# Factors prepared one ring entry at a time, and last sums that go on from copies in their banks

## The chip, the cores and the metric

The kernel runs on one core of one Trainium2 chip. The metric is the time of one execution on the device in microseconds (us). TensorE (PE in the profile, PEld its weight loads) multiplies matrices into PSUM, which has eight banks of 128 partitions by 512 float32; VectorE (DVE) and ScalarE (ACT) do elementwise work; SyncE (SP) issues the loads from HBM into SBUF.

## The reference

A decoder trunk of two layers over 256 positions, width 2048, all in float32: layer 0 mixes with a gated short convolution, layer 1 with latent attention of 16 heads. Behind each mixer stands an MLP with a squared ReLU, and every sub-layer is followed by a layer norm of the scaled input plus its result. What matters here are the two MLPs and the last norm:

```python
def sq_relu_mlp(x, w1, w2):
    return jnp.square(jax.nn.relu(x @ w1)) @ w2
...
    h = layer_norm(ALPHA * h + mix, ln_g[layer, 0], ln_b[layer, 0])
    h = layer_norm(ALPHA * h + sq_relu_mlp(h, mlp_w1[layer], mlp_w2[layer]), ln_g[layer, 1], ln_b[layer, 1])
```

w1 is 2048 x 8192 and w2 is 8192 x 2048 in each layer.

## The kernel before

**Factors and their ring.** A weight is used as two parts, hi and lo: ScalarE rounds the float32 value to float32r (hi), VectorE subtracts (lo = value - hi), and TensorE multiplies with both. split (L127, L128) does this for one *unit* of 128 x 1024 values. Units live in a ring of eight (the pool whl, tags hi and lo, WA = 8); the raw values are loaded into a ring of five (raws, RAW = 5; each load is issued at L138 on SP's queue). A unit of either ring can be filled again when its last reader has finished.

**The stream.** All weights stand in one list, stream, in the order of use. A *plain* entry is one unit: one load, one hi, one lo. A *paired* entry serves seven products that stand for eight (a Strassen scheme on two by two blocks) and is three units, prepared by prepare(i) in this order: unit 1 from the first load; unit t from differences of the two loads (raw_t, L160; its parts are hi_t and lo_t); unit 2 from the second load after L163 has put a difference into half of it; and then a half unit t4 (L166 and a split into t) in buffers of its own. FACTORS gives the order of the seven products (numbered 3, 1, 5, 7, 2, 6, 4): the first two read unit 1, the next two unit t, the next two unit 2, the last t4. Each is one dot: three matmuls at L290, L292 and L293, of which L292 reads lo.

**How far ahead.** take() hands out the next entries and first prepares those ahead, as long as their units, counted from the entries handed out, come to no more than LOOK = 5 (in one place LOOK + 1). It is called in the order of the program, ahead of the matmuls that use the entry. What is called earlier in the program is ranked higher, but the order of the instructions in each engine's queue is fixed when the kernel is built, by a planner that plays the program through with its own estimates: among the instructions that are ready at its time on an engine it takes the one that stands first in the program. In the queue each engine then keeps that order.

**One MLP.** The 8192 hidden columns are done in eight stages q of eight chunks of 128 (m = 0 to 7). In each, products computes x @ w1 for the chunks (names ps_u, L205 and L209), hidden applies ReLU and square (whole, L348; L704, L705) and splits the result into h; then the stage's part of h @ w2 follows. In q = 0 and q = 7 that is down (ps_d): all plain entries. In q = 1 to 6, the *fast* stages, it is down_pairs: three paired entries s0, s1, s2, then two plain ones p0 and p1 (all of these into ps_r), then four paired entries f0 to f3 (into ps_f). forms holds the sums of h blocks that the paired products need.

**Sums.** The running sums of h @ w2 lie in SBUF (acc, and sums for the four products named in OWN). In a fast stage a sum is copied into its bank by ScalarE (resumed, L605), TensorE accumulates onto it, and ScalarE copies it back (put_back, L609). Around the end of p1 these copies stand in the program so: put_back of the products 1, 5, 7 and 6 and resumed of 3 and 1 before the call of take for p0; resumed of 5 and 7 and put_back of 2 and 4 between that call and the call for p1; put_back of 22 and 3 behind the matmuls of p1. In q = 1 the four products of OWN start anew, so that resumed makes no copy for them. At q = 7 fold adds sums into acc while products runs.

**The end.** In q = 7 of the last MLP, down does the output blocks n = 0 and 1 and down_late the blocks 2 and 3, first for the rows t = 0, then for t = 1. For each (n, t) the bank is added to block(n, t) of acc (put, L592); finished then takes statistics of the row (bn_stats, L1025) and, after the last block, normalises: mean, variance and its root, centred (L1039), scaled (L1042), and for t = 1 three offsets from TensorE (L1053, L1058), whose banks Banks.next() draws from a count modulo eight. store sends the result to HBM.

Of the kernel before, what the change touches and what calls it, by code (L numbers as in the profile page):

```python
# [22 lines left out]
NQ = 8  # L23
# [11 lines left out]
NB = 4  # L35
# [18 lines left out]
def trunk(ctx: ExitStack, tc: tile.TileContext, xT, vecs, lead, w_first, w_in, w_out, w_kv, w_q, w_uk, w_uv,  # L54
# [66 lines left out]

    state = {"split": 0, "next": 0}
    ready = {}
# [17 lines left out]
    def prepare(i):  # L141

        if len(stream[i]) == 1:
            raw = load_raw(i, stream[i][0])
            hi, lo = ready[i] = parts(i)
            split(hi, lo, tiled(raw))
            return
        r1, r2 = (load_raw(f"{i}_{j}", src) for j, src in enumerate(stream[i]))
        out = []

        def finished(r, name):
            hi, lo = parts(name)
            split(hi, lo, tiled(r))
            out.append((hi, lo))

        b22, (b21, b12) = r1[:, BW:], (r2[:, :BW], r2[:, BW:])
        finished(r1, f"{i}_1")
        t = raws.tile([P, 1024], F32, tag="raw", name=f"raw{i}_t")
        two = "p (a c) -> p a c"
        nc.vector.tensor_tensor(t.rearrange(two, a=2), b12.unsqueeze(1).to_broadcast([P, 2, BW]),  # L160
                                r1.rearrange(two, a=2), ALU.subtract)
        finished(t, f"{i}_t")
        nc.vector.tensor_tensor(b12, b22, t[:, :BW], ALU.subtract)  # L163
        finished(r2, f"{i}_2")
        t4 = r1[:, :BW]
        nc.vector.tensor_tensor(t4, b21, b12, ALU.subtract)  # L166
        f = state["fast"].tile([P, 2, BW], F32R, tag="t4", name=f"t4_{i}", bufs=2)
        split(f[:, 0, :], f[:, 1, :], t4)
        b1, t13, b2 = ([[v.rearrange("p b c -> p (b c)")[:, o:o + BW] for v in w] for o in (0, BW)] for w in out)
        ready[i] = {"11": b1[0], "22": b1[1], "21": b2[0], "T2": b2[1], "T1": t13[0], "T3": t13[1],  # L170
                    "T4": [f[:, 0, :], f[:, 1, :]]}

    def size(i):

        return 1 if len(stream[i]) == 1 else 3

    def take(halves=2, look=LOOK):

        i = state["next"]
        state["next"] += halves  # L180
        ahead = -sum(size(j) for j in range(i, i + halves))
        for j in range(i, len(stream)):
            ahead += size(j)
            if ahead > look:
                break
            if j >= state["split"]:
                prepare(j)
                state["split"] = j + 1
        return [ready.pop(i + j) for j in range(halves)]

# [111 lines left out]

    def down(x, put, n, banks=(None, None), amid=None):

        ps = [psum("ps_d", bank) for bank in banks]
        for j in range(len(x) // 2):
            w, = take(1)
            for kk in range(2):
                k = 2 * j + kk
                for t in range(2):  # L310
                    dot(ps[t], wide_rows(w, kk), held(x[k], t), k == 0, k == len(x) - 1)
            if amid and 2 * j + 2 == len(x) // 2:
                amid()
        for t in range(2):
            put(n, t, ps[t])

    def down_late(x, put, blocks):

        ws = {}
        for t in range(2):  # L320
            for n in blocks:
                ps = psum("ps_d")
                for k in range(len(x)):
                    if (n, k // 2) not in ws:
                        ws[n, k // 2], = take(1)
                    dot(ps, wide_rows(ws[n, k // 2], k % 2), held(x[k], t), k == 0, k == len(x) - 1)
                put(n, t, ps)
# [196 lines left out]
    for k0, k1 in pieces:  # L524
# [5 lines left out]
        for u in range(HEAD):  # L530
            hi, lo = ready[2 * u + half]
            split(hi[:, at, :], lo[:, at, :], w[:, :, u, :])
    state["split"] = 2 * HEAD
    nc.sync.dma_start(vec, vecs)
# [32 lines left out]

    def mlp(idx, ln, blocks, fast, begin=None, extra=None):

# [92 lines left out]
        def fold():  # L662
# [3 lines left out]
            for d, a, b in ((c[:, 0, 0], c[:, 0, 0], s1), (s6, s6, s1), (c[:, 0, 1], c[:, 0, 1], s6), (s7, s7, s6),  # L666
# [3 lines left out]
                yield  # L670

        busy, free = (0, 1, 2, 3), (4, 5, 6, 7)
        for q in range(NQ):
# [54 lines left out]
            else:  # L728
                folds = fold()
                begun = {}  # L730
                for m, ps in enumerate(products(QC, xhl, TURNED, busy)):
# [6 lines left out]
                    if q == NQ - 1:  # L738
                        next(folds, None)
                        if begin:  # L740
                            begin(range(max(2 * m, 1), 2 * m + 2))

            if q == NQ - 1:
                blocks(block, put, h)
                return
# [261 lines left out]

    def to_out(block, put, h):
        gbt = act.tile([P, NB, 2 * BW], F32, tag="b", name="gbt")
# [13 lines left out]
        def finished(n, t, ps):  # L1023
            put(n, t, ps)
            nc.vector.bn_stats(out=stats[:, t, n, :], in_=block(n, t))  # L1025
            if n < NB - 1:
                if t == 1:
                    nc.vector.tensor_tensor(block(n, t), block(n, t), gbt[:, n, :BW], ALU.mult)
                return
# [7 lines left out]
            def centred(i):  # L1037
                us[i] = scratch(i)
                nc.vector.scalar_tensor_tensor(us[i], block(i, t), mv[:, 0:1], gbt[:, i, :BW], ALU.subtract, ALU.mult)  # L1039

# [22 lines left out]
        for n in range(2):  # L1063
            down(h, finished, n)
        down_late(h, finished, range(2, NB))

    with tc.tile_pool(name="fast2", bufs=1) as fast:
        mlp(3, after, to_out, fast, extra=turn_residual)
    Banks.close(banks)
# [94 lines left out]
```

## Time and profile before

| | |
|---|---|
| median of 3 runs (lowest to highest) | 2004.91 us (2004.71 to 2005.23) |
| the profiled execution, its own time | 2005.16 us |
| its span, first to last instruction | 2003.4 us |
| mean granted TensorE clock | 0.999 |
| busy share: PE, PEld, DVE, ACT | 100%, 87%, 86%, 67% |
| one fast stage, products of q = 3 to products of q = 4 | 83.65 us (621.65 to 705.30) |
| last matmul into the sums to the end of the span | 11.2 us (from 1992.24) |

A row of a profile view names line, engine, operation and tiles as out<-in; the number behind x is a count, and an arrow in brackets gives the idle time of the engine just before and what ended it. Rows in order of time begin with the start and the duration in us; where several alike follow one another they are merged (x3). Rows of stretches give the bounds, the length, and the busy time of each engine with its number of instructions.

### The profile page before, as it was taken

Reading aid. Unit: us, or ns where it says so; the run is one execution under the profiler, and the core shown is the slowest. Engines: PE = TensorE matmul, PEld = TensorE weight load, DVE = VectorE, ACT = ScalarE, POOL = GpSimd, SP = SyncE. Lnnn points to the kernel's source line nnn. Section 1 sums busy time; section 2 is a strip of 40 time slices with the busy share of each in tenths; the row PEclk is TensorE's granted clock in tenths of the full one; section 3 lists DMA queues with packets and bytes.
Section 4 is the critical chain, followed back from the end, with each engine's and each line's share of the span. In section 5 each row is a group of like instructions: output and inputs, shape, how many; then the busy total and the mean of one; then the engine's idle time right before and its main releaser. Section 6 shows DMA issues by size and latency. Waiting matters only on the chain.

```text
span 2003.4 us, 30132 instructions
## 1 busy us (share of the span) xinstructions
PE 1993.4 (100%) x11114; PEld 1737.5 (87%) x11114; DVE 1715.7 (86%) x2565; ACT 1347.5 (67%) x2142; POOL 2.3 (0%) x21
## 2 busy tenths in 40 slices
PE   9999999999999999999999999999999999999998
PEld 8888888988888888888889998898888888888886
DVE  8667667788999999989978988777899999999986
ACT  6444445586877787877756755558677778887771
POOL 0000000000000000000000000000000000000000
PEclk9999999999999999999999999999999999999999
DMA  8666666564647465574854543656464646656483
GB/s 314 210 189 188 188 190 189 184 193 146 223 164 244 147 231 197 187 247 133 281 173 158 170 140 128 195 183 196 147 233 147 233 159 219 218 181 231 152 276 118
DMA packets 106851, 385.84 MB, mean 193 GB/s; under 512 B 11856, under 2 KB 12624, under 8 KB 106448
## 3 DMA queue, kind: packets, MB, share of 16 engines
q1 hardware_dynamic: 106560, 383.79, 58.8%
q8 instruction: 87, 1.43, 0.3%
q14 instruction: 60, 0.49, 0.1%
q10 hardware_dynamic: 144, 0.13, 0.0%
HBM read 381.78 MB, written 2.10 MB: 192 GB/s over the span
## 4 chain that ended last, share of the span: by engine, by line
PE 90%; DVE 7%; issue 2%; ACT 1%; DMA 0%; DVEq 0%
PE ps_u L205 21%; PE ps_l L205 13%; PE ps_u L209 11%; PE ps_l L209 7%; PE ps_r L292 4%; PE ps_r L290 4%; PE ps_r L293 4%; PE ps_d L292 3%; PE ps_d L290 3%; PE ps_d L293 3%; DVE lo L128 2%; PE ps_w L239 2%; PE ps_w L238 2%; DVE lo_t L128 2%; PE ps_w L237 2%
## 5 line engine op out<-in xcount | busy, mean ns | idle before, releaser
L128 DVE TENSOR_TENSOR lo<-raw,hi 128x1024 fp32r<-128x1024 f32 x710 | 860.5, 1219 | 191.1 <-ACT hi L127 109.4
L127 ACT CAST hi<-raw 128x1024 fp32r<-128x1024 f32 x710 | 742.3, 1051 | 241.4 <-PE ps_l L205 97.5
L205 PE MATMUL ps_u<-xhl,hi 128*128 128x512 f32 x1792 | 622.8, 393 | 0.0
L209 PE MATMUL ps_u<-xhl,lo 128*128 128x256 f32 x1792 | 498.6, 280 | 0.0
L205 PEld LDWEIGHTS ps_u<-xhl,hi 128*128 128x128 f32 x1792 | 334.5, 187 | 74.2 <-ACT acc L588 0.2
L209 PEld LDWEIGHTS ps_u<-xhl,lo 128*128 128x128 f32 x1792 | 338.2, 189 | 1.7
L205 PE MATMUL ps_l<-xhl_a,hi 128*128 128x512 f32 x704 | 244.1, 393 | 0.0
L209 PE MATMUL ps_l<-xhl_a,lo 128*128 128x256 f32 x704 | 195.4, 279 | 0.0
L205 PEld LDWEIGHTS ps_l<-xhl_a,hi 128*128 128x128 f32 x704 | 132.1, 188 | 29.9
L127 ACT CAST hi_t<-raw_t 128x1024 fp32r<-128x1024 f32 x84 | 88.6, 1055 | 84.6 <-DVE raw_t L160 69.0
L209 PEld LDWEIGHTS ps_l<-xhl_a,lo 128*128 128x128 f32 x704 | 131.9, 188 | 0.2
L160 DVE TENSOR_TENSOR raw_t<-raw,raw 128x1024 f32<-128x1024 f32 x84 | 102.2, 1217 | 2.9 <-DMA raw<-in_w2f_dram 2.9
L128 DVE TENSOR_TENSOR lo_t<-raw_t,hi_t 128x1024 fp32r<-128x1024 f32 x84 | 102.3, 1218 | 1.4 <-ACT hi_t L127 0.9
L290 PE MATMUL ps_d<-hi,h 128*128 128x512 f32 x256 | 99.9, 390 | 0.0
L292 PE MATMUL ps_d<-lo,h 128*128 128x512 f32 x256 | 99.7, 389 | 0.0
L293 PE MATMUL ps_d<-hi,h 128*128 128x512 f32 x256 | 99.7, 389 | 0.0
L205 PE MATMUL ps_l<-z,hi 128*128 128x512 f32 x240 | 82.4, 391 | 0.0
L239 PE MATMUL ps_w<-xd,hi 128*128 128x258 f32 x256 | 72.8, 284 | 0.0
L237 PE MATMUL ps_w<-xd,hi 128*128 128x258 f32 x256 | 72.3, 282 | 0.0
L238 PE MATMUL ps_w<-xd,lo 128*128 128x258 f32 x256 | 72.3, 282 | 0.0
L205 PE MATMUL ps_l<-oT,hi 128*128 128x512 f32 x208 | 71.3, 391 | 0.0
L704 ACT ACTIVATE fp<-fp 128x256 f32<-128x256 f32 x96 | 40.0, 417 | 43.9 <-DVE fp L348 43.1
(286 smaller groups left out, 3890.5 us busy)
## 6 DMA issues: line engine op xcount, KB each, us to landing
raw<-in_w_dram SPq DMA_DIRECT2D x344, 512.0 KB, 4.5
raw<-in_w2f_dram SPq DMA_DIRECT2D x168, 512.0 KB, 4.0
raw<-in_w_in_dram SPq DMA_DIRECT2D x88, 512.0 KB, 4.2
raw<-in_w_out_dram SPq DMA_DIRECT2D x32, 512.0 KB, 3.7
raw<-in_w_o_dram SPq DMA_DIRECT2D x32, 512.0 KB, 4.1
raw<-in_w_kv_dram SPq DMA_DIRECT2D x10, 512.0 KB, 4.3
raw<-in_w_q_dram SPq DMA_DIRECT2D x8, 512.0 KB, 4.2
raw<-in_w_uk_dram SPq DMA_DIRECT2D x8, 512.0 KB, 3.9
```

The lines of the kernel that those rows point to most:

```text
L127: nc.scalar.copy(hi, src)
L128: nc.vector.tensor_tensor(lo, src, hi.bitcast(F32), ALU.subtract)
L160: nc.vector.tensor_tensor(t.rearrange(two, a=2), b12.unsqueeze(1).to_broadcast([P, 2, BW]), r1.rearrange(two, a=2), ALU.subtract)
L205: nc.tensor.matmul(ps, w[blk // 8][0][:, blk % 8, :], x, start=first, stop=False)
L209: nc.tensor.matmul(ps[:, :T], w[blk // 8][1][:, blk % 8, :], x[:, :T], start=False, stop=last)
L237: nc.tensor.matmul(ps[:, :W], hi, x[k][:, :W], start=k == 0, stop=False)
L238: nc.tensor.matmul(ps[:, :W], lo, x[k][:, :W], start=False, stop=False)
L239: nc.tensor.matmul(ps[:, :W], hi, x[k][:, W:], start=False, stop=k == NC - 1)
L290: nc.tensor.matmul(ps, x[0], w[0], start=first, stop=False, skip_group_check=onto)
L292: nc.tensor.matmul(ps[:, at], x[0], w[1][:, at], start=False, stop=False, skip_group_check=onto)
L293: nc.tensor.matmul(ps, x[1], w[0], start=False, stop=last, skip_group_check=onto)
L704: nc.scalar.activation(f, f, AF.Relu)
```

## The change

Two edits are made at once.

*One unit at a time.* prepare becomes a generator that stops after each of an entry's three units, and take counts units, not entries: it lets an entry begin whose first one or two units still fit under LOOK, and goes on with it at the next calls. Plain entries are prepared as before. The order in which units and loads are allotted stays the same.

*Last sums.* In q = 7 of the last MLP, ScalarE copies the blocks of acc into the banks of their last sums (last_sum): those of n = 0 with chunk 6, of n = 1 with chunk 7, and of n = 2 and 3 behind chunk 7. down and down_late then accumulate onto them, put is no longer called there, and finished reads the banks themselves, for the statistics and in centred. The eight sums take all eight banks. The arguments banks and amid of down, which no call uses, go.

```diff
--- before.py
+++ after.py
@@ -119,7 +119,7 @@
             cls.count += 1
             return (cls.count - 1) % (4 if cls.more is None else 8)
 
-    state = {"split": 0, "next": 0}
+    state = {"next": 0}
     ready = {}
 
     def split(hi, lo, src):
@@ -144,6 +144,7 @@
             raw = load_raw(i, stream[i][0])
             hi, lo = ready[i] = parts(i)
             split(hi, lo, tiled(raw))
+            yield
             return
         r1, r2 = (load_raw(f"{i}_{j}", src) for j, src in enumerate(stream[i]))
         out = []
@@ -155,11 +156,13 @@
 
         b22, (b21, b12) = r1[:, BW:], (r2[:, :BW], r2[:, BW:])
         finished(r1, f"{i}_1")
+        yield
         t = raws.tile([P, 1024], F32, tag="raw", name=f"raw{i}_t")
         two = "p (a c) -> p a c"
         nc.vector.tensor_tensor(t.rearrange(two, a=2), b12.unsqueeze(1).to_broadcast([P, 2, BW]),
                                 r1.rearrange(two, a=2), ALU.subtract)
         finished(t, f"{i}_t")
+        yield
         nc.vector.tensor_tensor(b12, b22, t[:, :BW], ALU.subtract)
         finished(r2, f"{i}_2")
         t4 = r1[:, :BW]
@@ -169,10 +172,13 @@
         b1, t13, b2 = ([[v.rearrange("p b c -> p (b c)")[:, o:o + BW] for v in w] for o in (0, BW)] for w in out)
         ready[i] = {"11": b1[0], "22": b1[1], "21": b2[0], "T2": b2[1], "T1": t13[0], "T3": t13[1],
                     "T4": [f[:, 0, :], f[:, 1, :]]}
+        yield
 
     def size(i):
 
         return 1 if len(stream[i]) == 1 else 3
+
+    begun = {}
 
     def take(halves=2, look=LOOK):
 
@@ -180,13 +186,17 @@
         state["next"] += halves
         ahead = -sum(size(j) for j in range(i, i + halves))
         for j in range(i, len(stream)):
-            ahead += size(j)
-            if ahead > look:
-                break
-            if j >= state["split"]:
-                prepare(j)
-                state["split"] = j + 1
-        return [ready.pop(i + j) for j in range(halves)]
+            for step in range(size(j)):
+                ahead += 1
+                if ahead > look:
+                    return [ready.pop(i + k) for k in range(halves)]
+                if j < 2 * HEAD:
+                    continue
+                steps = begun.setdefault(j, [prepare(j), 0])
+                if steps[1] == step:
+                    next(steps[0])
+                    steps[1] += 1
+        return [ready.pop(i + k) for k in range(halves)]
 
     def psum(name, bank=None):
 
@@ -300,30 +310,28 @@
 
         return [v[:, 4 * kk:4 * kk + 4, :].rearrange("p a c -> p (a c)") for v in w]
 
-    def down(x, put, n, banks=(None, None), amid=None):
-
-        ps = [psum("ps_d", bank) for bank in banks]
+    def down(x, put, n, sums=None):
+
+        ps = [sums[n, t] if sums else psum("ps_d") for t in range(2)]
         for j in range(len(x) // 2):
             w, = take(1)
             for kk in range(2):
                 k = 2 * j + kk
                 for t in range(2):
-                    dot(ps[t], wide_rows(w, kk), held(x[k], t), k == 0, k == len(x) - 1)
-            if amid and 2 * j + 2 == len(x) // 2:
-                amid()
+                    dot(ps[t], wide_rows(w, kk), held(x[k], t), k == 0 and not sums, k == len(x) - 1, onto=bool(sums))
         for t in range(2):
             put(n, t, ps[t])
 
-    def down_late(x, put, blocks):
+    def down_late(x, put, blocks, sums):
 
         ws = {}
         for t in range(2):
             for n in blocks:
-                ps = psum("ps_d")
+                ps = sums[n, t]
                 for k in range(len(x)):
                     if (n, k // 2) not in ws:
                         ws[n, k // 2], = take(1)
-                    dot(ps, wide_rows(ws[n, k // 2], k % 2), held(x[k], t), k == 0, k == len(x) - 1)
+                    dot(ps, wide_rows(ws[n, k // 2], k % 2), held(x[k], t), False, k == len(x) - 1, onto=True)
                 put(n, t, ps)
 
     OWN = ("1", "5", "7", "6")
@@ -530,7 +538,6 @@
         for u in range(HEAD):
             hi, lo = ready[2 * u + half]
             split(hi[:, at, :], lo[:, at, :], w[:, :, u, :])
-    state["split"] = 2 * HEAD
     nc.sync.dma_start(vec, vecs)
 
     zt = act.tile([P, NC, 2 * T], F32R, tag="b", name="z")
@@ -565,7 +572,7 @@
     ln.widen("a1", "a2")
     summed(ln, chain(products(1, z), lagged(NC - 1, z)), residual)
 
-    def mlp(idx, ln, blocks, fast, begin=None, extra=None):
+    def mlp(idx, ln, blocks, fast, begin=None, extra=None, last=False):
 
 
 
@@ -669,6 +676,13 @@
                 nc.vector.tensor_tensor(d, a, b, ALU.add)
                 yield
 
+        finals = {}
+
+        def last_sum(n, t, bank):
+
+            finals[n, t] = psum("ps_e", bank)
+            nc.scalar.copy(finals[n, t], block(n, t))
+
         busy, free = (0, 1, 2, 3), (4, 5, 6, 7)
         for q in range(NQ):
             ht = act.tile([P, QC, 2 * T], F32R, tag="c", name=f"h{idx}_{q}")
@@ -737,9 +751,17 @@
                         resume(busy, free, begun, m)
                     if q == NQ - 1:
                         next(folds, None)
+                        if last and m >= QC - 2:
+                            for t in range(2):
+                                last_sum(m - QC + 2, t, free[2 * (m - QC + 2) + t])
                         if begin:
                             begin(range(max(2 * m, 1), 2 * m + 2))
 
+            if q == NQ - 1 and last:
+                for i, (n, t) in enumerate(((2, 0), (3, 0), (2, 1), (3, 1))):
+                    last_sum(n, t, busy[i])
+                blocks(block, finals, h)
+                return
             if q == NQ - 1:
                 blocks(block, put, h)
                 return
@@ -1005,7 +1027,7 @@
             nc.tensor.transpose(ps[:, j * P:(j + 1) * P], xres[:, 4 * n + j, t * P:(t + 1) * P], id_t)
         nc.vector.scalar_tensor_tensor(block(n, t), ps, ALPHA, block(n, t), ALU.mult, ALU.add)
 
-    def to_out(block, put, h):
+    def to_out(block, finals, h):
         gbt = act.tile([P, NB, 2 * BW], F32, tag="b", name="gbt")
         for n in range(NB):
             nc.sync.dma_start(gbt[:, n, :], gb[n].partition_broadcast(P))
@@ -1021,11 +1043,10 @@
             return raws.tile([P, 1024], F32, tag="raw", name=f"u{i}")[:, :BW]
 
         def finished(n, t, ps):
-            put(n, t, ps)
-            nc.vector.bn_stats(out=stats[:, t, n, :], in_=block(n, t))
+            nc.vector.bn_stats(out=stats[:, t, n, :], in_=ps)
             if n < NB - 1:
                 if t == 1:
-                    nc.vector.tensor_tensor(block(n, t), block(n, t), gbt[:, n, :BW], ALU.mult)
+                    nc.vector.tensor_tensor(block(n, t), ps, gbt[:, n, :BW], ALU.mult)
                 return
             mv = small.tile([P, 2], F32, tag="nm", name="mv")
             nc.vector.bn_aggr(out=mv, in_=stats[:, t, :, :])
@@ -1036,7 +1057,7 @@
 
             def centred(i):
                 us[i] = scratch(i)
-                nc.vector.scalar_tensor_tensor(us[i], block(i, t), mv[:, 0:1], gbt[:, i, :BW], ALU.subtract, ALU.mult)
+                nc.vector.scalar_tensor_tensor(us[i], finals[i, t], mv[:, 0:1], gbt[:, i, :BW], ALU.subtract, ALU.mult)
 
             def scaled(i, x, other, op=ALU.add):
                 nc.vector.scalar_tensor_tensor(block(i, t), x, r, other, ALU.mult, op)
@@ -1061,11 +1082,11 @@
                 scaled(i, block(i, t), ps, ALU.subtract)
 
         for n in range(2):
-            down(h, finished, n)
-        down_late(h, finished, range(2, NB))
+            down(h, finished, n, finals)
+        down_late(h, finished, range(2, NB), finals)
 
     with tc.tile_pool(name="fast2", bufs=1) as fast:
-        mlp(3, after, to_out, fast, extra=turn_residual)
+        mlp(3, after, to_out, fast, extra=turn_residual, last=True)
     Banks.close(banks)
```

## The prediction

> **What bounds the kernel now.** The page came first, for the engines; then the busy time by stretches, one stretch for each run of paired products; then the waits of TensorE; then ScalarE and VectorE in order of time around one such run.
>
> ```profile
> PE 1993.4 (100%) x11114; PEld 1737.5 (87%) x11114; DVE 1715.7 (86%) x2565; ACT 1347.5 (67%) x2142; POOL 2.3 (0%) x21
> ```
>
> The profiled execution took 2005.16 us, its span and the time around it together; the sum below is made against that. It stands 0.25 us above the median of the three runs (2004.91). TensorE looks full, but ends of matmuls are modelled, so a short stall hides in its busy time. The length of a stretch doesn't hide it. In each of the twelve fast stages (q = 1 to 6 of two MLPs) a last run of four paired entries, f0 to f3 below, gives the same 84 matmuls into ps_f. The next view has one row for each stage, cut from the first matmul of that run to the first of the next stage; the first column after the bounds is the length.
>
> ```profile
> core 0: us, PE busy (x) PEld busy (x) DVE busy (x) ACT busy (x) POOL busy (x), PEclk, DMA share, GB/s
> 517.79:536.83 19.04, 19.04 (x85) 15.77 (x84) 18.92 (x21) 13.53 (x19) 0.00 (x0) 1.00 0.51 169
> 601.02:621.65 20.63, 19.61 (x85) 15.69 (x84) 19.37 (x21) 14.91 (x21) 0.00 (x0) 1.00 0.50 164
> 685.84:705.30 19.46, 19.33 (x85) 15.69 (x84) 19.32 (x21) 13.75 (x19) 0.00 (x0) 1.00 0.47 143
> ...
> 936.83:957.87 21.04, 19.78 (x86) 15.59 (x85) 19.57 (x22) 15.32 (x22) 0.00 (x0) 1.00 0.51 167
> 1464.44:1483.48 19.04, 19.04 (x86) 15.77 (x84) 18.80 (x21) 13.43 (x19) 0.00 (x0) 1.00 0.53 167
> ...
> 1633.03:1652.72 19.69, 19.34 (x86) 15.69 (x84) 19.38 (x21) 13.98 (x20) 0.00 (x0) 1.00 0.44 143
> ...
> sum 235.69, PE 232.18 PEld 188.32 DVE 231.34 ACT 167.55 POOL 0.00; mean PE 19.35 PEld 15.69 DVE 19.28 ACT 13.96 POOL 0.00
> ```
>
> Both q = 1 stages take 19.04 us: 84 matmuls at 0.227 us, no stall. The other ten are longer at the same granted clock (1.00): all twelve lose 235.69 - 12 x 19.04 = 7.21 us. Three rows give 1.59 (601), 2.00 (936) and 0.65 (1633); the other seven share 7.21 - 4.24 = 2.97, 0.42 each as in the row of 685. VectorE is busy for 19.3 us of these 19.46: the run is paced by it.
>
> ```profile
> PEld ps_f L292 <- DVE lo_t L128: 7.5, 11, 1.3
> ```
>
> What TensorE waits for is a low part of the middle unit of an entry (lo_t). The two next views, of ScalarE and of VectorE, show what made it late in the stage of the row of 685.
>
> ```profile
> 680.73 1.55 ACT L609 COPY sums<-ps_r 128x512 f32<-128x512 f32 x3
> 682.16 1.65 ACT L605 COPY ps_f<-sums 128x512 f32<-128x512 f32 x3
> 683.72 1.09 ACT L609 COPY acc<-ps_r 128x512 f32<-128x512 f32 x2
> 684.67 1.08 ACT L127 CAST hi<-raw 128x1024 fp32r<-128x1024 f32 x1
> ...
> 686.58 1.08 ACT L127 CAST hi<-raw 128x1024 fp32r<-128x1024 f32 x1
> 687.53 1.10 ACT L609 COPY acc<-ps_r 128x512 f32<-128x512 f32 x2
> ```
>
> ```profile
> 682.27 1.22 DVE L160 TENSOR_TENSOR raw_t<-raw,raw 128x1024 f32<-128x1024 f32 x1
> 683.52 0.69 DVE L163 TENSOR_TENSOR raw<-raw,raw_t 128x512 f32<-128x512 f32 x1
> 685.79 1.22 DVE L128 TENSOR_TENSOR lo<-raw,hi 128x1024 fp32r<-128x1024 f32 x1 [1.57 <-PE ps_r L292]
> ...
> 700.72 1.22 DVE L128 TENSOR_TENSOR lo_t<-raw_t,hi_t 128x1024 fp32r<-128x1024 f32 x1
> ```
>
> ScalarE does eight copies on end between 680.73 and 684.67, and only then the first high part of f1 (hi at 684.67), although f1's raw data had landed: VectorE read it for raw_t at 682.27. VectorE then idles 1.57 us before f1's first low part (685.79) and works without a gap until the lo_t of f3, at 700.72. That one ends near 701.9; the run's 71st matmul, the first to read it, is due at 685.84 + 70 x 0.227 = 701.7.
>
> The q = 1 stage is an experiment that the kernel makes on itself: there sums has no earlier contents, so the three copies ps_f<-sums don't exist.
>
> ```profile
> 513.48 0.60 ACT L605 COPY ps_f<-acc 128x512 f32<-128x512 f32 x1
> 514.00 0.60 ACT L609 COPY acc<-ps_r 128x512 f32<-128x512 f32 x1
> 514.48 1.07 ACT L127 CAST hi<-raw 128x1024 fp32r<-128x1024 f32 x1
> ```
>
> ```profile
> 515.70 1.22 DVE L128 TENSOR_TENSOR lo<-raw,hi 128x1024 fp32r<-128x1024 f32 x1
> ...
> 530.50 1.22 DVE L128 TENSOR_TENSOR lo_t<-raw_t,hi_t 128x1024 fp32r<-128x1024 f32 x1
> ```
>
> Here f1's first high part starts 3.31 us before the run (514.48 against 517.79), not 1.17 us before it; lo follows with no idle, f3's lo_t starts at +12.71 us instead of +14.88, and nothing stalls.
>
> **Part 1, take and prepare.** Work, matmuls and bytes stay; only places in the program move. Before, take began an entry of three units only if all three fit in LOOK; now single units of it begin. Counting through take, these move one call earlier: the first unit of s0 (to the call of m = 5), the first two of s1 (to m = 7), of s2 (to s0), of f1 (to the first plain entry of the run, p0), of f2 (to f0) and of f3 (to f1). Each brings its two loads on SP's queue, its casts on ScalarE and its subtractions on VectorE; the order of loads among themselves doesn't change.
>
> Five of the six moves I cost at nothing. Between the calls of s0 and s1, f0 and f1, f1 and f2 the program has matmuls only, so the units of s2, f2 and f3 pass no other instruction of ScalarE, VectorE or SP. The moves of s0 and s1 pass the work on hidden chunks 5 and 7, but there the ring of eight sets the time, not the place:
>
> ```profile
> 666.12 1.06 ACT L127 CAST hi_t<-raw_t 128x1024 fp32r<-128x1024 f32 x1 [1.42 <-PE ps_u L205]
> ```
>
> For this cast (s2's middle unit) ScalarE stands idle until TensorE gives back a ring unit at the end of chunk 7, and s1's two units, three and four places earlier in the ring, had theirs before. Without that cover VectorE would do them ahead of chunk 7, whose h is first read by p0, three entries of 21 x 0.227 = 4.76 us after the products.
>
> The move of f1 counts. It passes the second and third ps_f<-sums (products 5 and 7 of f0) and the two copies acc<-ps_r of 683.72: four copies, (684.67 - 682.16) - 0.55 = 1.96 us. The cast of 684.67 then starts near 682.7 and ends near 683.7; VectorE's lo goes on behind L163, at 684.2, and 1.57 us of idle time goes. Some comes back: the cast of f1's third unit (686.58) has the same work in front of it as now, so VectorE, earlier than now, waits about 0.5 us for it (684.2 + two lows of 1.14 + 0.65 for L166 = 687.1, against 687.6). I take 1.1 us earlier for f3's lo_t; the bounds are 0 and 1.57. Gain: 2.97 + 0.65 + 1.1 + 1.1 = **5.82 us**; bounds 0 and 7.21.
>
> What is late next: the passed copies. Products 5 and 7 are the third and fourth factor of f0, due 6 and 9 matmuls into the run, at 687.2 and 687.9; behind two casts (1.9 us) they end near 685.2 and 685.7. Bank by bank it goes on like that; the tightest is factor 4, which needs the bank of the first copy of 687.53, due at 685.84 + 18 x 0.227 = 689.9. In the stage of 936 these are narrower:
>
> ```profile
> 934.72 1.64 ACT L605 COPY ps_f<-sums 128x512 f32<-128x512 f32 x3
> ...
> 940.08 1.10 ACT L609 COPY acc<-ps_r 128x512 f32<-128x512 f32 x2
> ```
>
> Product 7 would end at 936.36 + 1.9 = 938.3, due at 938.87; factor 4's bank comes free at 940.6 now, due at 940.92, and a cast of 0.5 us slipped in front would cost 0.2 to 0.3 there. That lies inside my bounds.
>
> **Part 2, the last sums.** Eight adds of VectorE (L592) go and eight copies of ScalarE (L605) come; TensorE's matmuls stay as they are. Only the last add lies on the end:
>
> ```profile
> 1992.66 0.69 DVE L592 TENSOR_TENSOR acc<-acc,ps_d 128x512 f32<-128x512 f32 x1 [1.24 <-PE ps_d L293]
> 1993.38 0.69 DVE L1025 BATCH_NORM_STATS2 stats<-acc 128x6 f32<-128x512 f32 x1
> ```
>
> It takes the chain 0.72 us (1992.66 to 1993.38). In the changed kernel the statistics, and the centring behind them, read the bank directly. No row has that; L592 reads a bank in the same 0.69 us in which the statistics read SBUF, and the slowest reader of a bank is this one, whose 0.82 us each hold waits for TensorE too:
>
> ```profile
> 1997.55 2.47 DVE L1042 SCALAR_TENSOR_TENSOR acc<-acc,rr,offset 128x512 f32<-128x512 f32 x3 [0.56 <-PE offset L1058]
> ```
>
> I take the first row: **0.7 us** gained. Bounds: 0.72 - 2 x (0.82 - 0.69) = 0.46, and 0.8, since nothing excludes a shorter read. [...]
>
> The eight copies, some 4.6 us, are hidden: in that stage ScalarE idles before each cast.
>
> ```profile
> 1957.30 1.05 ACT L127 CAST hi<-raw 128x1024 fp32r<-128x1024 f32 x1 [1.67 <-PE ps_d L293]
> ```
>
> The first two are issued with chunk 6 and needed a chunk and a half later. Without that cover the first matmul of the last projection would wait some 0.6 us once. The sums now hold all eight banks; the three offsets of the end take banks 2, 3 and 4, as before, whose sums, (3,0), (2,1) and (1,1), have been read by then.
>
> **Sum.** 2005.16 - 5.82 - 0.7 = 1998.6 for a profiled execution, 0.25 less for the median: **1998.4 us**.
>
> **The rivals.** About 0.2% (4 us) is what a measurement of this kernel can tell from no change.
>
> *A, the order stays or VectorE waited for the ring.* The row of 685.79 names TensorE (ps_r), not ScalarE; if a ring unit was the last to come, an earlier cast gains nothing, and only part 2 is left: 2004.2 us. Against it: in the stage of 601 the same wait is put down to the cast, and at q = 1 the same unit was free 2.1 us before the run.
>
> ```profile
> 602.14 1.23 DVE L128 TENSOR_TENSOR lo<-raw,hi 128x1024 fp32r<-128x1024 f32 x1 [1.33 <-ACT hi L127]
> ```
>
> [...]
>
> *B, slower: the passed copies hold up the start of f0.* ScalarE's queue is in order: if f1's second cast stands in it ahead of the copies for products 5 and 7 and waits for VectorE's raw_t, all copies wait. It decides from 2.0 us of delay beyond mine in a usual stage (687.2 against 685.2), 0.5 us in that of 936. Were it 3 us, a usual stage would stall 1.0 us instead of 0.42 and that of 936 2.5 instead of 2.0; 0.55 more in each of ten is 2004.91 + 5.5 - 0.7 = 2009.7 us. Against it: raw_t ended at 683.5, before that cast's turn.
>
> *C, all stalls go.* 2004.91 - 7.21 - 0.72 = 1997.0 us. It needs 1.6 and 2.0 us of VectorE's time in the stages of 601 and 936, more than the idle time in the row above (1.33).
>
> **How the numbers follow.** Forecast 0.58, C 0.08, A 0.20, B 0.14. The forecast's own range is 1997 to 2001 (0.5 us earlier instead of 1.1 still gives 2.97 + 3 x 0.5 + 0.7 = 5.2 us). To leave out no more than 2 in 10 the range must take in A: 1996.8 to 2004.5. Faster by over 0.2% are forecast and C, 0.66; within it A, 0.20; slower B, 0.14.
>
> **What would show it.** The ten long runs into ps_f shrink to 19.04 us, those of 601 and 936 to about 19.5 and 20; the wait of ps_f for lo_t falls from 7.5 to under 2 us; in a stage as that of 685 f1's first cast stands before the second copy ps_f<-sums, and VectorE's idle before f1's low is under 0.6 us. At the end L592 is gone from the last projection, and the statistics start where the add starts now, right behind the last matmul into the sums. I am wrong if the runs keep their lengths, if a new wait for ACT ps_f L605 shows up on TensorE, or if the stretches of products, or of s0 to p1, lengthen.

## The result and the profile after

| | before | changed |
|---|---|---|
| median of 9 runs (lowest to highest) | 2004.71 us (2003.03 to 2006.03) | 1999.25 us (1997.46 to 2001.39) |
| profiled execution, its own time | 2005.16 us | 1997.46 us |
| its span | 2003.4 us | 1995.7 us |
| twelve runs into ps_f, sum | 235.69 us | 228.56 us |
| last matmul into the sums to the end of the span | 11.2 us | 10.4 us (1985.26 to 1995.7) |

The ratio of the changed kernel to the one before is 0.9974, 95% interval 0.9965 to 0.9983: 5.46 us faster. The two profiled executions lie further apart, 7.7 us, since the one of the changed kernel was the fastest of its nine.

The busy line of the page first, then the busy time by stretches, one for each run into ps_f, cut as before.

```profile
PE 1990.0 (100%) x11114; PEld 1738.8 (87%) x11114; DVE 1710.9 (86%) x2557; ACT 1352.5 (68%) x2150; POOL 2.3 (0%) x21
```

```profile
601.17:620.21 19.04, 19.04 (x86) 15.77 (x84) 18.97 (x22) 15.10 (x22) 0.00 (x0) 1.00 0.53 173
684.39:703.43 19.04, 19.04 (x85) 15.77 (x84) 18.78 (x22) 15.10 (x21) 0.00 (x0) 1.00 0.57 170
...
934.07:953.11 19.04, 19.04 (x85) 15.77 (x84) 18.97 (x22) 15.10 (x23) 0.00 (x0) 1.00 0.52 173
...
1878.41:1897.54 19.13, 19.13 (x86) 15.69 (x84) 19.06 (x21) 15.18 (x23) 0.00 (x0) 1.00 0.54 179
sum 228.56, PE 228.56 PEld 189.15 DVE 226.86 ACT 177.74 POOL 0.00; mean PE 19.05 PEld 15.76 DVE 18.90 ACT 14.81 POOL 0.00
```

The page's shares say almost nothing: PE 100% in both, VectorE 86% in both, eight instructions moved from VectorE to ScalarE. The lengths say it all: eleven of the twelve runs take 19.04 us (19.03 in one), also those that took 20.63 and 21.04 before. 7.13 of the 7.21 us of stalls are gone. The rest of the execution gets no longer: 2005.16 - 235.69 = 1769.47 us before, 1997.46 - 228.56 = 1768.90 us after.

The waits of TensorE's weight loads, longest in total first:

```profile
PEld offset L1079 <- DVE udiag L1077: 1.3, 1, 1.3
PEld warm L372 <- DVE col L373: 1.0, 1, 1.0
```

No wait for lo_t is left; what leads the list are waits at the kernel's end and start. (The one run of 19.13 us has a wait of 0.2 us for a copy back into acc.) ScalarE and VectorE in order of time around the run that begins at 684.39 (the stage of the row of 685.84 before):

```profile
680.57 0.62 ACT L612 COPY ps_f<-sums 128x512 f32<-128x512 f32 x1
681.09 1.08 ACT L127 CAST hi<-raw 128x1024 fp32r<-128x1024 f32 x1
682.04 1.07 ACT L127 CAST hi_t<-raw_t 128x1024 fp32r<-128x1024 f32 x1
682.99 1.13 ACT L612 COPY ps_f<-sums 128x512 f32<-128x512 f32 x2
684.03 1.10 ACT L616 COPY acc<-ps_r 128x512 f32<-128x512 f32 x2
684.99 1.08 ACT L127 CAST hi<-raw 128x1024 fp32r<-128x1024 f32 x1
...
686.46 1.11 ACT L616 COPY acc<-ps_r 128x512 f32<-128x512 f32 x2
```

```profile
680.24 1.22 DVE L162 TENSOR_TENSOR raw_t<-raw,raw 128x1024 f32<-128x1024 f32 x1
...
682.20 1.23 DVE L128 TENSOR_TENSOR lo<-raw,hi 128x1024 fp32r<-128x1024 f32 x1
683.34 1.22 DVE L128 TENSOR_TENSOR lo_t<-raw_t,hi_t 128x1024 fp32r<-128x1024 f32 x1
684.48 0.69 DVE L169 TENSOR_TENSOR raw<-raw 128x512 f32<-128x512 f32 x1
685.08 1.22 DVE L162 TENSOR_TENSOR raw_t<-raw,raw 128x1024 f32<-128x1024 f32 x1
686.22 1.22 DVE L128 TENSOR_TENSOR lo<-raw,hi 128x1024 fp32r<-128x1024 f32 x1
...
696.89 1.22 DVE L128 TENSOR_TENSOR lo_t<-raw_t,hi_t 128x1024 fp32r<-128x1024 f32 x1
```

ScalarE's first two casts for f1 (681.09, 682.04) stand ahead of the second copy ps_f<-sums and of acc<-ps_r: four copies are passed. f1's first low part starts 2.19 us before the run (682.20 against 684.39), not 0.05; VectorE has no idle time in front of it; f3's lo_t starts at +12.50 us (696.89 - 684.39), not at +14.88.

At the end of the kernel, TensorE's last matmul into the sums and VectorE behind it:

```profile
1985.26 0.39 PE L303 MATMUL ps_e<-hi,h 128*128 128x512 f32 x1
...
1985.69 0.70 DVE L1046 BATCH_NORM_STATS2 stats<-ps_e 128x6 f32<-128x512 f32 x1 [2.83 <-PE ps_e L303]
...
1986.79 0.74 DVE L1060 SCALAR_TENSOR_TENSOR u<-ps_e,mv,gbt 128x512 f32<-128x512 f32 x1
```

The add is gone, and the statistics start 0.43 us after the start of the last matmul, where the add started before (1992.66 - 1992.24 = 0.42).

### The profile page after: what moved, and what is told of

Same layout as the page of the kernel before. It is cut to its first block, busy times and chain, and to the rows that moved or that the text cites. A ratio compares the mean times of both kernels' runs of the same rounds, so it can differ in the third digit from the quotient of the medians.

```text
span 1995.7 us, 30183 instructions
## 1 busy us (share of the span) xinstructions
PE 1990.0 (100%) x11114; PEld 1738.8 (87%) x11114; DVE 1710.9 (86%) x2557; ACT 1352.5 (68%) x2150; POOL 2.3 (0%) x21
## 4 chain that ended last, share of the span: by engine, by line
PE 100%; DVE 0%; issue 0%; DVEq 0%
PE ps_u L215 21%; PE ps_l L215 13%; PE ps_u L219 11%; PE ps_l L219 7%; PE ps_r L303 4%; PE ps_r L300 4%; PE ps_r L302 4%; PE ps_f L300 4%; PE ps_f L303 4%; PE ps_f L302 4%; PE ps_d L300 2%; PE ps_d L303 2%; PE ps_d L302 2%; PE ps_w L249 2%; PE ps_w L248 2%; PE ps_w L247 2%
## 5 line engine op out<-in xcount | busy, mean ns | idle before, releaser
L300 PE MATMUL ps_d<-hi,h 128*128 128x512 f32 x192 | 75.0, 391 | 0.0
L303 PE MATMUL ps_d<-hi,h 128*128 128x512 f32 x192 | 74.8, 389 | 0.0
L302 PE MATMUL ps_d<-lo,h 128*128 128x512 f32 x192 | 74.8, 389 | 0.0
```

The costliest lines, as they stand in the source:

```text
L300: nc.tensor.matmul(ps, x[0], w[0], start=first, stop=False, skip_group_check=onto)
L302: nc.tensor.matmul(ps[:, at], x[0], w[1][:, at], start=False, stop=False, skip_group_check=onto)
L303: nc.tensor.matmul(ps, x[1], w[0], start=False, stop=last, skip_group_check=onto)
```

## The experiments

Theory: f1's first casts stood behind four copies in ScalarE's queue, this paced VectorE up to f3's lo_t, and the change lets them pass. Rivals: the gain comes from the other five moves or from the ring; or from part 2. Each ratio below is to the kernel before, with its 95% interval.

**The two parts by themselves.** The edit of *units_alone* keeps prepare and take as changed and takes the end back:

```diff
-        ps = [sums[n, t] if sums else psum("ps_d") for t in range(2)]
+        ps = [psum("ps_d", bank) for bank in banks]
...
-                ps = sums[n, t]
+                ps = psum("ps_d")
```

> Part 1 alone: entries prepared one unit at a time, the last sums as before. My theory (part 1 takes away the stall at the end of the fast stages, part 2 an add of 0.72 us at the end): all twelve runs into ps_f 19.04 us long, and 4.5 to 5 us off the median, 0.7 less than the whole change. Rival (part 2 does more than its add, for instance by giving VectorE time in the last stage): at most 3.5 us off.

*sums_alone* is the other half, the kernel before with the new end:

```diff
-                ps = psum("ps_d")
+                ps = sums[n, t]
...
+            nc.scalar.copy(finals[n, t], block(n, t))
```

> Part 2 alone: last sums go on from copies, entries prepared whole. My theory: 0.7 us off the median, hardly to be told from none, and in the profile the statistics start where the add started, 0.72 us off the way from the last matmul to the end; runs into ps_f 19.46 us and longer as before. Rival (part 2 brings a good part of the gain): 2 us off or more.

Measured, beside 2004.65 for the kernel before: units_alone 1999.64 us, 0.9976 (0.9967 to 0.9986); sums_alone 2004.2 us, 0.9998 (0.9990 to 1.0007). Part 1 carries the gain. Part 2's 0.45 us can't be told from nothing by the times; in the trace of the whole change it is 0.71 us of the chain at the end (from the start of the last matmul to the start of the statistics: 1993.38 - 1992.24 = 1.14 us before, 0.43 after). In the profile of units_alone not all twelve runs take 19.04 us, as had been expected: three take 19.21, 19.53 and 19.88 us, and TensorE waits there for copies back into acc.

**Which of the six moves.** Both of these kernels are units_alone with one more condition in take, which is called with LOOK + 1 for p0 and p1 alone. *f1_alone* lets an entry begin in part only there:

```diff
         for j in range(i, len(stream)):
+            if look == LOOK and ahead + size(j) > look:
+                break
             for step in range(size(j)):
```

> Part 1 with one of its six moves only: an entry may begin in part at the call for p0 (that is f1), at every other call only whole. My theory (f1's first casts pass four copies on ScalarE, the other moves do nothing): the same as part 1 alone, 4.5 to 5 us off, every run into ps_f 19.04 us, VectorE's idle before f1's first low gone. Rival (the moves of f2 and f3 count too, since VectorE fills its time with them): runs of 601 and 936 keep 0.3 to 1 us of stall, 3 to 4 us off.

*all_but_f1* does it everywhere else:

```diff
         for j in range(i, len(stream)):
+            if look > LOOK and ahead + size(j) > look:
+                break
             for step in range(size(j)):
```

> Part 1 without the move of f1: at the calls of p0 and p1 an entry begins only whole, at all other calls unit by unit. My theory: no gain, the runs into ps_f 19.4 to 21 us as before, the first cast of f1 behind eight copies, VectorE idle 1.3 to 1.6 us before f1's first low. Rival (units of s1, s2, f2 or f3 being earlier is what helps): 2 us off or more, with runs shorter than before.

Measured: f1_alone 1999.92 us, 0.9976 (0.9966 to 0.9986); all_but_f1 2004.81 us, 1.0000 (0.9992 to 1.0009). The move of f1 alone brings what part 1 brings, and the five others bring nothing that the times resolve. The stretches of the runs into ps_f, first of f1_alone:

```profile
600.01:621.45 21.44, 19.63 (x85) 15.62 (x84) 21.34 (x24) 17.48 (x25) 0.00 (x0) 1.00 0.55 178
685.64:704.68 19.04, 19.04 (x86) 15.77 (x84) 18.97 (x21) 15.33 (x22) 0.00 (x0) 1.00 0.57 171
...
852.09:872.07 19.98, 19.53 (x85) 15.61 (x84) 19.91 (x23) 15.91 (x23) 0.00 (x0) 1.00 0.56 183
```

and of all_but_f1:

```profile
685.00:704.47 19.47, 19.34 (x85) 15.69 (x84) 19.33 (x21) 13.75 (x19) 0.00 (x0) 1.00 0.45 142
```

Without f1's move the runs stay at the 19.47 us of before; with it the usual ones take 19.04. But four runs of f1_alone are long in this profile, which is of the slowest of its nine executions, and the longest run, at 600.01, is worth a look. TensorE, then ScalarE:

```profile
601.14 0.39 PE L305 MATMUL ps_f<-hi,h 128*128 128x512 f32 x1
602.88 0.50 PE L302 MATMUL ps_f<-hi_t,forms 128*128 128x512 f32 x1 [1.35 <-ACT ps_f L616]
```

```profile
599.70 0.61 ACT L616 COPY ps_f<-sums 128x512 f32<-128x512 f32 x1
600.22 1.06 ACT L127 CAST hi<-raw 128x1024 fp32r<-128x1024 f32 x1
601.30 1.05 ACT L127 CAST hi_t<-raw_t 128x1024 fp32r<-128x1024 f32 x1
602.25 1.10 ACT L616 COPY ps_f<-sums 128x512 f32<-128x512 f32 x2
```

Here the whole queue is late (f1's first cast at +0.21 us of the run, not at -3.30 as at 681.09 above), and product 5's copy, passed by two casts, is what TensorE waits for: (602.88 - 601.14) - 0.23 = 1.51 us. That is what rival B of the prediction feared, a passed copy that comes too late. The step that B named for it, the second cast waiting for raw_t, is hardly there: this cast starts 1.08 us after the first (601.30 - 600.22), against 0.95 at 681.09, so it waited 0.13 us.

**The whole of f1 at once.** *whole_f1* is the kernel before, with all three units of f1 begun at p0's call, so that all its casts pass the copies:

```diff
-                    w, = take(1, LOOK + 1)
+                    w, = take(1, LOOK + 2)
```

> The kernel before with one number changed: the calls for p0 and p1 look LOOK + 2 units ahead instead of LOOK + 1, so that f1 is prepared whole at p0's call; no entry is ever begun in part. My theory (what counts is that f1's casts stand ahead of the four copies on ScalarE, not the grain): a gain too, 3 to 5 us; but now f1's third cast and its half unit also stand ahead of copies, so TensorE waits more often for a bank of f0 (products 5, 7 or 4), 0.3 to 1.5 us in late stages. Rival (one unit at a time is what helps, by filling VectorE's gaps): at most 1.5 us off.

2001.38 us, 0.9985 (0.9976 to 0.9993), and this wait of TensorE:

```profile
PEld ps_f L290 <- ACT ps_f L605: 4.3, 8, 1.5
```

The order alone, with whole entries, gives 3.05 us (2004.43 - 2001.38), where the changed kernel beside it gains 4.69 us (2004.43 - 1999.74), part 2's 0.7 us among them. TensorE's waits are now for banks that the passed copies fill, eight of them; that they are the whole difference isn't shown. Giving out f1 by units keeps its third unit behind the four copies.

**Fewer units past the copies.** In the changed kernel, *look5* lets one unit of f1 begin at p0 and the second at p1, *one_unit* one at p0 and the others at p1:

```diff
-                    w, = take(1, LOOK + 1)
+                    w, = take(1)
```

```diff
-                    w, = take(1, LOOK + 1)
+                    w, = take(1, LOOK + (two[0][1] == "22"))
```

> The changed kernel with LOOK instead of LOOK + 1 at the calls for p0 and p1: one unit of f1 is begun at p0, the second at p1, the third at f0. Theory of the scatter (in late stages the changed kernel waits for the copies that f1's casts passed: product 5, and the bank of factor 4): f1's third cast and half unit now stand behind the last two copies, so TensorE never waits for a bank of f0; f3's lo_t comes later, within the slack of 1 us or more. Then the median falls by 0.5 to 1.5 us below the changed kernel's (1997.7 to 1998.7) and its spread narrows. Rival (the scatter comes from VectorE's lateness itself): runs into ps_f end on lo_t again, 0.4 us in usual stages, median 2001 or more.

> The changed kernel with LOOK at p0's call and LOOK + 1 at p1's: only the first unit of f1 passes the four copies, its second and third stand where f1 stood before. Theory of the scatter: ScalarE no longer waits for VectorE's raw_t of f1 ahead of the copies, so product 5 is in time; factor 4 can still wait by the third cast and the half unit. Median 1998 to 1999.5. Rival (the second unit is needed early): runs into ps_f of 19.3 us and more in usual stages, median 2001 or more.

> The changed kernel once more, for a second profile and for its scatter on the same chip as the others. My theory of the scatter (a load that lands late makes VectorE late in a stage, and when raw_t of f0 starts later than some 7.8 us before the run into ps_f, TensorE waits for a bank): median 1999 to 2000; in the profile any run longer than 19.04 us has its raw_t of f0 later than that, and waits for a copy (ACT, ps_f or acc), none for lo_t. Rival (late stages end on lo_t as before): the longer runs wait for DVE lo_t.

look5 2003.22 us, 0.9995 (0.9986 to 1.0004); one_unit 2002.98 us, 0.9991 (0.9982 to 1.0000); after_again, the changed kernel beside them, 1999.74 us, 0.9976 (0.9967 to 0.9985). The expectations for look5 and one_unit failed. That for after_again held for the median, but not for its "none for lo_t", as is shown further down. The waits of look5, then of one_unit:

```profile
PEld ps_f L302 <- DVE lo_t L128: 5.1, 10, 1.3
```

```profile
PEld ps_f L300 <- ACT acc L616: 4.1, 6, 1.3
PEld ps_f L302 <- DVE lo_t L128: 3.9, 7, 0.6
```

I had taken f1's first unit for the one that counts. It isn't the only one. The cast of the second unit now stands behind the copies, and VectorE waits for it, in a usual stage of look5 like this:

```profile
685.38 1.23 DVE L128 TENSOR_TENSOR lo_t<-raw_t,hi_t 128x1024 fp32r<-128x1024 f32 x1 [0.67 <-ACT hi_t L127]
```

In one_unit the same wait takes 0.41 to 0.94 us. The stall for lo_t returns in all ten stages of look5 and in seven of one_unit, where factor 4's bank (ACT acc) is late as well in six.

**The third unit behind the last copies.** after_again's profile had long runs too, three of which wait for factor 4's bank. So *third_late* leaves the first two units as in the changed kernel and puts the third behind the put_backs of 22 and 3, which free factor 4's bank:

```diff
-                    w, = take(1, LOOK + 1)
+                    w, = take(1, LOOK + (two[0][1] == "2"))
```

> The changed kernel, but f1's third unit (f1_2's cast) is prepared behind the last two put_backs, those that fill factor 4's bank, while its first two units still pass. Theory: the stall at factor 4's bank, 0.9 us in three stages of a profile, goes, and in late stages f3's lo_t takes its place, since the third unit is now about 1 us later on ScalarE: the same as the changed kernel within 0.5 to 1 us, 1998.5 to 2000.5. Rival (factor 4's bank is all that is left to gain): 1.5 us less than the changed kernel, 1998. Rival (every unit of f1 is needed early, as with five units of lead): 3 us more, 2003.

2004.07 us, 0.9998 (0.9989 to 1.0007): missed again, on the side of the last rival.

```profile
PEld ps_f L302 <- DVE lo_t L128: 6.7, 9, 1.3
PEld ps_f L300 <- ACT ps_f L612: 2.5, 3, 1.6
```

The wait for factor 4's bank (ACT acc) is gone, lo_t is back in nine stages, and in the two that begin latest a copy into a bank (L612) comes late. No version of mine beats the changed kernel. But the place of the third unit explains only a part of this loss, as the table at the end of this section shows.

**More copies in the way.** The last test puts a dose on the queue: products 5 and 7 are copied into their banks twice, once in the kernel before (*before_double*, ahead of f1's casts) and once in the changed one (*after_double*, behind the first two of them):

```diff
+                            if q != FAST[0]:
+                                for p in "57":
+                                    nc.scalar.copy(then[p], place(p, 0))
```

> The kernel before, but the copies of the resumed products 5 and 7 into their banks are made twice, with the same data, in all fast stages but the first. So two more copies of about 0.52 us stand on ScalarE ahead of the first cast of f1. Theory (ScalarE's order sets when f3's lo_t is there): the run of f0 to f3 begins no earlier and lo_t comes 1.0 us later, so the usual runs are 20.5 us in place of 19.46; over some ten stages the time rises by about 10 us, to 2015. Rival (the stall was for the ring or for TensorE itself, ScalarE's order is only beside it): no more than 2 us, 2004 to 2006.

> The changed kernel with the same two copies doubled. Here they stand behind the two casts of f1's first unit. Theory: f1's casts and with them f3's lo_t keep part of their lead, but factor 4's bank, filled after these copies, comes 1.0 us later, which is about what it had to spare in the usual stages: usual runs 19.05 to 19.4 us, late ones about 1 us longer than without; +2 to +6 us, 2002 to 2006, a much smaller price than that of the same copies in the kernel before. Rival (position on ScalarE does not matter, the engine's sum of work does): the same price as in the kernel before, +10 us.

before_double 2014.58 us, 1.0044 (1.0030 to 1.0059), 10.0 us above the 2004.56 of the kernel before, as expected; after_double 2003.93 us, 0.9999 (0.9990 to 1.0008), 4.2 to 4.7 us above the changed kernel's two medians. The same two copies, 1.04 us of ScalarE in ten stages, cost 1.0 us of each stage on average where they stand ahead of f1's casts and under half of it where they stand behind. The work added to ScalarE is the same in both; the place counts. VectorE in a usual stage of before_double, at f1's first low part and at f3's lo_t:

```profile
687.95 1.23 DVE L128 TENSOR_TENSOR lo<-raw,hi 128x1024 fp32r<-128x1024 f32 x1 [2.62 <-ACT hi L127]
...
702.88 1.22 DVE L128 TENSOR_TENSOR lo_t<-raw_t,hi_t 128x1024 fp32r<-128x1024 f32 x1
```

The idle time is 2.62 us instead of 1.57, and lo_t starts 15.92 us into the run (702.88 - 686.96) instead of 14.88: the 1.04 us of the two copies come through whole. Whole stages, from products to products, first of before_double and then of the kernel before:

```profile
707.03:792.00 84.97, 84.75 (x430) 71.05 (x429) 79.33 (x103) 67.38 (x105) 0.00 (x0) 1.00 0.62 198
```

```profile
705.30:788.95 83.65, 83.53 (x430) 71.20 (x429) 79.10 (x103) 66.53 (x103) 0.00 (x0) 1.00 0.61 201
```

A usual stage grows by 1.3 us with ScalarE at 67.38 and VectorE at 79.33 of 84.97 us busy, so neither's total sets it; TensorE has the same 430 matmuls in both. One caution: with the longer wait the planner also moved a few matmuls of f3 ahead of the one that reads lo_t, so that in before_double the stall stands at f3's casts and not at lo_t. In after_double it stands where the passed copies are:

```profile
PEld ps_f L300 <- ACT acc L616: 5.7, 10, 0.9
PEld ps_f L300 <- ACT ps_f L660: 2.2, 4, 0.9
```

**One length for all of them.** VectorE's chain can be measured in every profile, from the start of f0's raw_t to the start of f3's lo_t; the medians over the ten stages with q of 2 to 6:

| kernel | chain on VectorE |
|---|---|
| before_double | 25.3 us |
| before, all_but_f1 | 24.2 us |
| sums_alone | 24.0 us |
| look5 | 23.8 us |
| one_unit | 23.0 us |
| after_double | 22.6 us |
| third_late | 22.4 us |
| changed (both profiles), units_alone, f1_alone, whole_f1 | 22.0 us |

This length follows what stands ahead of f1's casts. The time also depends on the waits for banks, as in whole_f1, whose chain is as short as the changed kernel's, and on how early a stage begins. third_late's chain is 0.4 us longer, under its loss of 4.3 us or more; nine of its ten stages also begin late, with f0's raw_t 5.6 to 7.9 us ahead of the run, where the changed kernel's first profile has 7.7 to 9.6. Whether its order brings that about isn't known.

## Why the prediction was right, and where it was off

**What bounds the kernel: right.** The excess lengths (7.21 us) were where the gain was, and their cause was a place in ScalarE's queue: f1_alone and all_but_f1 show it by keeping the move or taking it away, before_double by a dose. By busy share TensorE leads here (100%; its weight loads 87% and VectorE 86%, before and after), and the gain did come as shorter waits of TensorE. The shares did not show where: the order on an engine at 67%.

**Five moves at nothing: right.** all_but_f1 stands at 1.0000 (0.9992 to 1.0009).

**Part 1, the move of f1: right mechanism, mis-sized term.** The step that failed is "Some comes back", the 0.5 us that VectorE was to wait for f1's third unit. The planner had work for that gap: between lo_t at 683.34 and lo at 686.22 VectorE does L169 and, new there, raw_t of f2 (685.08), without a pause. Also raw_t of f1 itself started 0.58 us earlier against the run (680.24 - 684.39 = -4.15; before 682.27 - 685.84 = -3.57). With the idle time of 1.57 us this is 2.15 us at f1's first low part, and 2.38 at f3's lo_t, where I had 1.1 and a bound of 1.57. Of the 2.38, 0.27 is a stage that began earlier (f0's raw_t 9.61 us ahead of the run, before 9.34); VectorE's chain itself is 2.1 us shorter here and, against the 23.66 us that it took in the stages of 601 and 936, 1.7 us shorter there. That covers the 1.6 us of the run of 601. That the run of 936 lost its 2.0 us whole was luck: its stage began 8.21 us ahead in this execution, before 7.22, and in the second profile below, with 7.08, the run is long again. So the trace gained 7.13 us where the sum had 5.82: in this execution it is case C, which I had held to need more of VectorE's time than there was.

**Over many executions less than that.** The median moved by 5.46 us, near the forecast, but for a reason that the forecast had only as a bound. In the changed kernel's second profile:

```profile
767.73:787.42 19.69, 19.33 (x85) 15.69 (x84) 19.62 (x22) 15.76 (x23) 0.00 (x0) 1.00 0.56 182
...
934.84:954.68 19.84, 19.38 (x86) 15.63 (x85) 19.77 (x22) 15.90 (x23) 0.00 (x0) 1.00 0.57 186
...
1545.34:1565.85 20.51, 19.50 (x86) 15.68 (x84) 18.28 (x21) 14.23 (x21) 0.00 (x0) 1.00 0.49 152
...
sum 231.97, PE 229.89 PEld 188.77 DVE 227.73 ACT 177.74 POOL 0.00; mean PE 19.16 PEld 15.73 DVE 18.98 ACT 14.81 POOL 0.00
```

Three runs (767, 934 and 1630) wait for factor 4's bank, up to 0.9 us, which the prediction named as the tightest. There the stall has moved from VectorE's lo_t to the copies that were passed. So the effect that rival B feared exists in stages that begin late, at a small price: it takes back 0.65 + 0.80 + 0.55 = 2.0 us in this profile, not more than the gain. The run of 1545 waits for lo_t again, for another reason, a load that came late inside the run:

```profile
1555.85 1.05 ACT L127 CAST hi<-raw 128x1024 fp32r<-128x1024 f32 x1 [3.78 <-DMA raw<-in_w2f_dram]
```

VectorE then waits 2.16 us for this cast, and its chain takes 24.3 us in this stage.

**Part 2: right.** 0.7 us forecast, 0.71 in the trace, beneath what the times resolve. The eight copies, a median of 0.59 us each (0.588), hide: no wait of TensorE names them. The statistics took 0.70 us from the bank and 0.69 from SBUF before, the centring 0.74 from the bank; before, from SBUF, VectorE had this:

```profile
1994.48 0.74 DVE L1039 SCALAR_TENSOR_TENSOR u<-acc,mv,gbt 128x512 f32<-128x512 f32 x1
```

Over all their instructions in the two profiles the medians are 0.693 us from the bank and 0.690 from SBUF for the statistics (eight each), 0.742 and 0.741 for the centring (five each).

**The sum.** The two misses, a term 1.3 us too small and late stages that give some of it back, nearly cancel, and that they do is luck: 1998.4 was forecast, 1999.25 and 1999.74 were measured. Its sum for a profiled execution, 1998.6, lies 1.1 us above the one profiled; against the two medians the forecast was 0.9 and 1.3 us too low.

**What stays open.** Why some stages are late. In the 40 stages with q of 2 to 6 of units_alone, f1_alone and the changed kernel's two profiles, every run that f0's raw_t precedes by less than 7.8 us takes 19.10 us or more, and of the others only one does (1545, above). What I saw in one late stage is a load that came late at the stage's beginning; ScalarE in f1_alone, ahead of the run of 600:

```profile
550.87 1.05 ACT L127 CAST hi<-raw 128x1024 fp32r<-128x1024 f32 x1 [1.90 <-DMA raw<-in_w_dram]
```

and in the changed kernel, in the same stage, without a stall at its end:

```profile
548.62 1.05 ACT L127 CAST hi<-raw 128x1024 fp32r<-128x1024 f32 x1 [0.45 <-DMA raw<-in_w_dram]
```

That loads make stages begin late is seen in this one, not shown. A sixth buffer for raw values would be a test of it; no run here has one.

## What to carry to other kernels

Where an engine shows 100%, cut the trace into stretches of equal work and compare their lengths: here a first stage without three of the copies showed both what could be gained and why. On ScalarE a cast waited here for the copies ahead of it in the queue (two more of them, 1.04 us, put f3's lo_t 1.04 us later), so ask what stands ahead of the instruction that feeds the slow chain; moving it ahead of the copies gained 4.73 us here (2004.65 - 1999.92 in f1_alone), less in a stage where a passed copy was itself late (1.51 us of TensorE's time in that kernel's run of 600), and units small enough to go between them gained more than whole ones here, by 1 to 2 us (about 4.0 to 5.0 us without part 2 against 3.05, with intervals that overlap). Compare schedules by many executions: one profile of the changed kernel showed 7.1 us gained in these runs, the next 3.7 (235.69 - 231.97).

## What the runs showed of the hardware that I had not expected

Two profiles of the changed kernel, the same instructions in the same order, differ by 3.4 us of stalls (228.56 against 231.97) at a granted clock of 1.00 throughout: 2.0 us of the longer one's stalls stand in three stages that begin late, 1.5 us in one run whose cast waited 3.78 us for a load. Statistics and centring on 128 x 512 float32 cost VectorE the same from a bank as from SBUF, within 0.01 us (medians of 0.693 us in the changed kernel and 0.690 before, 0.742 and 0.741).
